# The order of TensorE's small products in two chunked recurrences: directions, heads and blocks in turn over the array's parts

## The chip, the core and the metric

The kernel runs on one core of one Trainium2 chip. The metric is the device time of one launch in microseconds (us). A launch is the whole inference step of a two-layer network, so every number below stands against a kernel of over 3 ms, of which the change touches one stage.

## The reference, cut to what matters

The reference takes 128 context tokens and 512 sample tokens of width 1024 through two layers. Layer 0 is SwiGLU, then a mixer with two parallel groups of heads (RWKV-7 with 8 heads of 64, and a gated DeltaNet with 4 heads of 128), then SwiGLU. Layer 1 has attention and a long convolution in the mixer's place. Both recurrences of layer 0 go over the tokens forwards and backwards, and the two outputs are added. All is fp32. RWKV's recurrence, and DeltaNet's with its triangular solve, are:

```python
def wkv7_scan(r, w, k, v, kk, a, S0):
    def step(S, xs):
        r_t, w_t, k_t, v_t, kk_t, a_t = xs
        sk = jnp.einsum('bhvk,bhk->bhv', S, kk_t)
        S = (S * w_t[:, :, None, :] - sk[..., None] * (kk_t * a_t)[:, :, None, :]
             + v_t[..., None] * k_t[:, :, None, :])
        return S, jnp.einsum('bhvk,bhk->bhv', S, r_t)
...
y_f, S_f = wkv7_scan(rh, hd(decay[:, :, 0]), hd(k_dir[:, :, 0]), vh, kk, hd(a[:, :, 0]), S0[:, 0])
y_b, S_b = wkv7_scan(fl(rh), fl(hd(decay[:, :, 1])), fl(hd(k_dir[:, :, 1])), fl(vh), fl(kk), ...)
y = y_f + fl(y_b)
...
T = lax.linalg.triangular_solve(eye + lower, jnp.broadcast_to(eye, lower.shape),
                                left_side=True, lower=True, unit_diagonal=True)
```

The kernel computes both in chunks of 64 tokens. Inside a chunk the step by step update becomes the inverse of a 64x64 unit triangular matrix (for every chunk, head and direction) and a few small matrix products; between chunks a state of 64x64 (RWKV) or 128x128 (DeltaNet) is carried.

## The kernel before, in words

**Layout.** 640 tokens are ten chunks of 64 (NCH = 10; CH = 64): two of context (PCH = 2), eight of sample. RWKV's heads go in four pairs: the two heads of a pair (hh = 0, 1) lie on partitions 0 to 63 and 64 to 127. A pair is worked on together with one DeltaNet head. Forward (d = 0) and backward (d = 1) go side by side: step s takes chunk c0 forwards and chunk c1 backwards. In the tiles that hold 64 tokens, direction 0 has one half of the partitions and direction 1 the other.

**TensorE's array and shapes.** All of the products here go through one helper, `mm` (L286–287), which is why the profile shows them all as L287; they are told apart by the names of their operands. The profile's row `ps<-VU,AT 64*64 64x64` is a product on a 64x64 part of the 128x128 array (64 rows hold the contraction, 64 columns the output's partitions), with 64 columns streamed. Which rows and which columns of the array follows from the partitions of the operands and of the output. An fp32 product is two weight loads and two MATMUL records. Results go to PSUM in banks of 128 x 512 words, and from there an engine copies them to SBUF. In this stage there are eight banks by tags (L962): two "ma", one "mt", one "mj", two "mc" (RWKV's steps), two "mg" (DeltaNet's steps).

**The functions that the change touches.**
- `rwkv_prep` (L1033), once for each head pair. At L1107–1115 it makes the lower triangular matrices L: 40 products of 64x64 (the profile's `w,w`), ten to a PSUM bank, four banks one after another, each masked by VectorE into L. A product's rows of the array are its head's half, its columns its direction's half.
- `inverses` (L1128), once for each head pair, as a generator in two parts. The 32x32 diagonal blocks are inverted by VectorE and GpSimd; the second part (L1185–1208) makes the off-diagonal blocks with 32x32 products: first `RL·rn` and `LT·gn` (the profile's `L,iv`/`iv,L` and `LT,gn`/`gn,LT`), a negated copy by ScalarE (zr, zg), then the products of zr and zg, and copies back by VectorE. RWKV's have ten products (chunks) for one 32x32 part of the array in a row, DeltaNet's have five.
- `rwkv_step` (L1244), for each of ten chunks of each pair: 40 steps. 36 of them have an incoming state S, four have none. Its parts: masked products AT (L1265–1268) and transposes E; then **AT·VU + Z·S** (L1281–1287), which is copied to B by VectorE for d = 0 and by ScalarE for d = 1; then **XT·B** (L1289–1293, the profile's `B,L`), copied to VU by ScalarE with a change of sign; then E·VU, which gives the new state S2 (L1295–1306); then the output **y** = Z·S + VU·AT (L1308–1321), added to ys. AT·VU uses 64 rows of the array (one direction's tokens) and 64 columns; Z·S uses all 128 rows (both heads, zeros in one of them) and 64 columns.

**What sets the order.** `mixers0` (L917–1015) writes the order of the stage out by hand: `advance((0,), n - LAP)`, `prepare(2)`, `advance((0, 1), LAP)`, `tail(0)`, and so on; `prepare` calls rwkv_prep, DeltaNet's preparation and the first part of `inverses`, and the second part of the pair before. The generator `chunks` (L1212) runs `gdn_step` (L1515, DeltaNet's step) and `rwkv_step` in turn, one part (up to a `yield`) of each. What that writes is not the last word: the kernel is built under `TileContext(nc, schedule_with_timeline_sim=True)` (L2143), a planner that orders each engine's instructions by a simulated timeline of its own. So the order in the trace can differ from the order in the code, and does: a product of DeltaNet stands between the two directions' blocks in some steps.

Of the kernel before, what the change touches and what calls it, by code (L numbers as in the profile page):

```python
# [9 lines left out]
ALU = mybir.AluOpType  # L10
# [3 lines left out]
P = 128  # L14
# [22 lines left out]
CH = 64  # L37
NCH = T // CH
# [220 lines left out]
class K:  # L259
# [773 lines left out]
    def rwkv_prep(self, hp, xp):  # L1033

        nc, I, ra = self.nc, self.I, self.ar
# [4 lines left out]
        r, k, kr, v = [self.wl() for _ in range(4)]  # L1040
# [6 lines left out]
        q = self.both(blk, sq, "ma")  # L1047
# [14 lines left out]
        L = self.t(xp, [P, 2 * NCH, CH], "L")  # L1062
        eG = self.t(xp, [P, 2, NCH], "eG")
        sa = []
        for d in range(2):
            sig, a = self.w(), self.w()
            for i, (b, out) in enumerate((("w0", sig), ("a0", a))):
                q = self.both(lora[:, 2 * i + d], self.wad[i], "ma")
                for c in range(2):
                    o = ch(out[:, c * H:c * H + H])  # L1070
# [3 lines left out]
        PQ, ks = [], []  # L1074
# [29 lines left out]
        at, _ = CONST["rmask"]  # L1104
        mask = self.const[:, at:at + CH].unsqueeze(1)
        n = NCH // 2
        for g in range(0, 2 * NCH, n):  # L1107
            hh, c0 = divmod(g, NCH)
            hr = slice(64 * hh, 64 * hh + 64)
            q = self.ps("ma")  # L1110
            for i in range(n):
                for d in range(2):
                    self.mm(q[64 * d:64 * d + 64, CH * i:CH * i + CH], PQ[d][1][hr, c0 + i], PQ[d][0][hr, c0 + i])
            nc.vector.tensor_tensor(out=L[:, g:g + n], in0=q[:, :n * CH].rearrange("p (u m) -> p u m", u=n),
                                    in1=mask.broadcast_to([P, n, CH]), op=ALU.mult)

        nc.vector.scalar_tensor_tensor(out=kds, in0=kds, scalar=self.col("r_k", hp), in1=r, op0=ALU.mult, op1=ALU.mult)
        q = self.both(blk, kds, "ma")
# [9 lines left out]
    def inverses(self, R, G):  # L1128
        nc, ra = self.nc, self.ar
        NP = NCH // 2  # L1130
        RL, LT = R["L"], G["LT"]
        g0, r0 = 4 * NP, 8 * NP
        nb = r0 + 8 * NCH
        dr = [self.t(self.dp, [nb, 32, 32], f"bl{i}") for i in range(3)]
        gv = lambda t, e: t[g0 * e:g0 * e + g0].rearrange("(b z c) s t -> b z s c t", b=2, z=2)
        rv = lambda t: t[r0:].rearrange("(b h c) s t -> b h s c t", b=2, h=2)
        quad = lambda hi, b: slice(64 * hi + 32 * b, 64 * hi + 32 * b + 32)
        cb = lambda b: slice(32 * b, 32 * b + 32)
        for b in range(2):
            for u in range(2):  # L1140
                nc.sync.dma_start(out=rv(dr[0])[b, u], in_=RL[quad(1 - u, b), :, cb(b)])
                for e in range(2):
                    nc.sync.dma_start(out=gv(dr[0], e)[b, u], in_=LT[quad(u, b), e, :, cb(b)])
        iv = lambda shape: self.t(ra, shape, "iv", bufs=4)
        L = [iv([nb, 16, 32]) for _ in range(2)]
        for i in range(2):
            nc.sync.dma_start(out=L[i][g0:], in_=dr[0][g0:, 16 * i:16 * i + 16])
        raw = [iv([g0, 16, 32]) for _ in range(2)]
        for i in range(2):
            nc.sync.dma_start(out=raw[i], in_=dr[0][:g0, 16 * i:16 * i + 16])  # L1150
        for i in range(2):
            for j in range(2):
                nc.scalar.copy(out=L[i][:g0, :, 16 * j:16 * j + 16], in_=raw[j].rearrange("p t s -> p s t")[:, 16 * i:16 * i + 16])
        xs = []
        for j0, nj, eng in ((0, NPOOL, nc.gpsimd), (NPOOL, 32 - NPOOL, nc.vector)):
            X = self.t(ra, [nb, nj, 32], f"X{j0}")
            flat = X.rearrange("p a b -> p (a b)")
            nc.gpsimd.memset(flat, 0.0)
            nc.gpsimd.memset(flat[:, j0::33], 1.0)
            self.invert_blocks(eng, L, X, j0, self.t(ra, [nb, 192], "inv", bufs=2))  # L1160
            nc.sync.dma_start(out=dr[1][:, j0:j0 + nj], in_=X)
            xs.append((X, j0))
        for i in range(2):
            xt = iv([nb, 16, 32])
            for X, j0 in xs:
                nc.scalar.copy(out=xt[:, :, j0:j0 + X.shape[1]], in_=X.rearrange("p s t -> p t s")[:, 16 * i:16 * i + 16])
            nc.sync.dma_start(out=dr[2][:, 16 * i:16 * i + 16], in_=xt)
        yield

        rn = iv([P, 2 * NCH, 32])  # L1170
        gn = self.t(ra, [P, NP, 32], "gn")
        for b in range(2):
            for u in range(2):
                nc.sync.dma_start(out=RL[quad(1 - u, b), :, cb(b)], in_=rv(dr[1])[b, u])
                for e in range(2):
                    nc.sync.dma_start(out=LT[quad(u, b), e, :, cb(b)], in_=gv(dr[2 - e], e)[b, u])
        for u in range(2):
            nc.sync.dma_start(out=rn[quad(1 - u, 0)], in_=rv(dr[2])[0, u])
            for e in range(2):
                nc.sync.dma_start(out=gn[quad(u, 1 - e)], in_=gv(dr[1 + e], e)[1 - e, u])  # L1180

        zr, zg = iv([P, 2 * NCH, 32]), self.t(ra, [P, NP, 32], "zg")
        qv = lambda q, rr, n, at=0: q[rr, at:at + 32 * n].rearrange("p (c s) -> p c s", c=n)
        qr, qg = [self.ps("ma") for _ in range(2)], self.ps("mt")
        for d in range(2):  # L1185
            for u in range(2):
                lo, hi = quad(u, 0), quad(u, 1)
                for c in range(NCH):
                    self.mm(qv(qr[d], hi, NCH)[:, c], RL[lo, NCH * d + c, 32:], rn[lo, NCH * d + c])
                nc.scalar.activation(out=zr[hi, NCH * d:NCH * d + NCH], in_=qv(qr[d], hi, NCH), func=AF.Copy, scale=-1.0)  # L1190
        for e in range(2):
            for z in range(2):
                lo, hi = quad(z, 1 - e), quad(z, e)
                for c in range(NP):
                    self.mm(qv(qg, hi, NP)[:, c], LT[lo, e, c, cb(e)], gn[lo, c])
        nc.scalar.activation(out=zg, in_=qv(qg, slice(None), NP), func=AF.Copy, scale=-1.0)
        for d in range(2):
            for u in range(2):
                lo, hi = quad(u, 0), quad(u, 1)
                for c in range(NCH):  # L1200
                    self.mm(qv(qr[d], lo, NCH)[:, c], zr[hi, NCH * d + c], RL[hi, NCH * d + c, 32:])
                nc.vector.tensor_copy(out=RL[lo, NCH * d:NCH * d + NCH, 32:], in_=qv(qr[d], lo, NCH))
        for e in range(2):
            for z in range(2):
                lo, hi = quad(z, 1 - e), quad(z, e)
                for c in range(NP):
                    self.mm(qv(qg, lo, NP, 32 * NP)[:, c], zg[hi, c], LT[hi, e, c, cb(e)])
                nc.vector.tensor_copy(out=LT[lo, e, :, cb(e)], in_=qv(qg, lo, NP, 32 * NP))
        yield

# [33 lines left out]
    def rwkv_step(self, X, ys, c0, c1, S, first):  # L1244

        nc, rt = self.nc, self.rt
        ZD, XD, XT, eG = [X[n] for n in ("ZD", "XD", "L", "eG")]
        ident = self.con("ident")
        pair = slice(c0, NCH + c1 + 1, NCH + c1 - c0)
        hrs = [slice(64 * hh, 64 * hh + 64) for hh in range(2)]  # L1250
        dc = [(0, c0), (1, c1)]
# [4 lines left out]
        Z, B = self.zeroed[self.zi % len(self.zeroed)]  # L1256
# [5 lines left out]
        mask = self.const[:, at:at + P].unsqueeze(1).broadcast_to([P, 4, P])  # L1262
        AT = self.t(rt, [P, 2, 2, P], "AT", bufs=3)
        q = self.ps("mj")
# [4 lines left out]
        q = self.ps("mj")  # L1269
# [4 lines left out]
        VU = self.t(rt, [P, 2, P], "VU", bufs=3)  # L1274
# [3 lines left out]
        for d, c, r, u in rows:  # L1278
            nc.scalar.copy(out=VU[r, d], in_=q[r, 2 * P:3 * P])
        yield  # L1280
        q = self.ps("mc")  # L1281
        for d, c, r, u in rows:
            for hh, hr in enumerate(hrs):
                self.mm(q[r, hr], AT[r, d, hh, :CH], VU[r, d, hr], stop=S is None)
                if S is not None:
                    self.mm(q[r, hr], Z[:, d, hh, :CH], S[:, d], start=False)
            (nc.vector.tensor_copy, nc.scalar.copy)[d](out=B[r, d], in_=q[r, :P])
        yield
        q = self.ps("mc")  # L1289
        for d, c, r, u in rows:  # L1290
            for hh, hr in enumerate(hrs):
                self.mm(q[u, hr], XT[:, NCH * hh + c], B[:, d, hr])
            nc.scalar.activation(out=VU[u, d], in_=q[u, :P], func=AF.Copy, scale=-1.0)
        S2 = self.t(rt, [P, 2, CH], "S", bufs=NSB)
        for d, c in dc:  # L1295
            yield
            q = self.ps("mc")
# [8 lines left out]
                nc.vector.scalar_tensor_tensor(out=S2[:, d], in0=q[:, :CH], scalar=e, in1=Se, op0=ALU.mult, op1=ALU.add)  # L1306
        yield
        q = self.ps("mc")  # L1308
        for hh, hr in enumerate(hrs):
            for d, c in dc:  # L1310
                o = q[hr, CH * d:CH * d + CH]
                if S is not None:
                    self.mm(o, S[:, d], Z[:, d, hh, CH:], stop=False)
                self.mm(o, VU[:, d, hr], AT[:, d, hh, CH:], start=S is None)
        for d, c in dc:
            to, x = ys[:, CH * c:CH * c + CH], q[:, CH * d:CH * d + CH]
# [830 lines left out]
```

## Time and profile before

| What | us |
|---|---|
| Median of three runs | 3269.26 |
| Fastest and slowest of them | 3264.29, 3270.95 |
| The profiled execution | 3277.03 |
| Its span in the profile | 3275.3 |
| Recurrence stage, looked at as a window of it | 900 to 1340 |

The profiled execution is one launch, 7.8 us above the median; durations from it are summed against its own time. TensorE's mean granted clock in it is 0.954 of full speed.

How to read the profile: PE is TensorE's MATMUL, PEld its weight loads, DVE is VectorE, ACT is ScalarE, POOL is GpSimd, SP the engine that issues DMAs. A row of a timeline gives the start, the length from the first start to the last end, engine, line, operation, out<-in by the program's names, the part of the array and the tile, and how many records were merged into it; in brackets the idle time before it and what ended it. The ends of MATMUL records are modelled and overlap the next record's start, so what one costs is read from its start to the next one's. A row of a window gives busy time and records of each engine and the granted TensorE clock. A row of a group gives the number of records, their busy time, the mean length in ns and the engine's idle time before them with what ended it.

### The profile page before, as it was taken

Reading aid. Unit: us, or ns where it says so; the run is one execution under the profiler, and the core shown is the slowest. Engines: PE = TensorE matmul, PEld = TensorE weight load, DVE = VectorE, ACT = ScalarE, POOL = GpSimd, SP = SyncE. Lnnn points to the kernel's source line nnn. Section 1 sums busy time; section 2 is a strip of 40 time slices with the busy share of each in tenths; the row PEclk is TensorE's granted clock in tenths of the full one; section 3 lists DMA queues with packets and bytes.
Section 4 is the critical chain, followed back from the end, with each engine's and each line's share of the span. In section 5 each row is a group of like instructions: output and inputs, shape, how many; then the busy total and the mean of one; then the engine's idle time right before and its main releaser. Section 6 shows DMA issues by size and latency. Waiting matters only on the chain.

```text
span 3275.3 us, 56038 instructions
## 1 busy us (share of the span) xinstructions
PE 3076.1 (94%) x21505; PEld 2751.9 (84%) x21505; DVE 2253.8 (69%) x3995; ACT 1378.2 (42%) x2876; POOL 1210.5 (37%) x1110
## 2 busy tenths in 40 slices
PE   7899999998899999889999979999989998899998
PEld 2799999987767777688999979999978846899998
DVE  5956667568567554586666787677766686877777
ACT  2423334676455444442333453333544423533333
POOL 4723334236424120153334555444410012544442
PEclk9999999999878888899999989999989998899999
DMA  7455433456444222426554232222321124222222
GB/s 261 160 187 179 161 127 97 157 167 169 132 119 112 66 77 69 141 96 204 163 167 149 71 98 96 78 85 84 93 94 54 58 75 163 71 95 80 78 91 81
DMA packets 277588, 385.37 MB, mean 118 GB/s; under 512 B 128704, under 2 KB 161120, under 8 KB 275400
## 3 DMA queue, kind: packets, MB, share of 16 engines
q1 hardware_dynamic: 277160, 381.13, 36.9%
q8 instruction: 169, 2.77, 0.3%
q14 instruction: 99, 0.81, 0.1%
q0 software_dynamic: 160, 0.66, 0.0%
HBM read 330.29 MB, written 51.42 MB: 117 GB/s over the span
## 4 chain that ended last, share of the span: by engine, by line
PE 58%; DVE 11%; DMA 3%; ACT 2%; issue 2%; POOL 1%; SPq 1%; DVEq 0%; ACTq 0%; POOLq 0%
PE ps L287 57%; DMA wr<-in_wd_dram 1%; DVE wl L655 1%; DVE b L605 1%; DVE wl L471 1%; DVE X L826 1%; DVE nx L539 0%; DMA wr<-in_wo_dram 0%; DVE inv L824 0%; PE ps L1750 0%; PE ps L1271 0%; POOL X L826 0%; DVE hidl L476 0%; DVE nacc L506 0%; POOL inv L824 0%
## 5 line engine op out<-in xcount | busy, mean ns | idle before, releaser
L287 PE MATMUL ps<-hh,wh 128*128 128x320 f32 x2208 | 695.6, 317 | 13.0 <-ACT hh L545 5.6
L287 PE MATMUL ps<-hl,wh 128*128 128x320 f32 x2208 | 692.1, 314 | 3.0 <-POOL hl L546 2.9
L287 PE MATMUL ps<-hh,wl 128*128 128x320 f32 x2208 | 681.9, 313 | 4.9 <-DVE wl L471 4.7
L287 PE MATMUL ps<-b,wh 128*128 128x320 f32 x2112 | 479.9, 314 | 39.4 <-DVE b L605 21.8
L287 PEld LDWEIGHTS ps<-hh,wh 128*128 128x128 f32 x2208 | 419.9, 191 | 28.1 <-issue 8.4
L287 PEld LDWEIGHTS ps<-hl,wh 128*128 128x128 f32 x2208 | 420.1, 190 | 8.0 <-POOL hl L546 4.4
L287 PEld LDWEIGHTS ps<-hh,wl 128*128 128x128 f32 x2208 | 417.7, 190 | 8.4 <-DVE wl L471 5.8
L287 PEld LDWEIGHTS ps<-b,wh 128*128 128x128 f32 x2112 | 360.2, 191 | 47.3 <-DVE b L605 23.8
L287 PE MATMUL ps<-hidl,wh 128*128 128x320 f32 x1248 | 383.2, 309 | 0.0
L287 PE MATMUL ps<-hidh,wh 128*128 128x320 f32 x1248 | 382.6, 312 | 0.0
L287 PE MATMUL ps<-hidh,wl 128*128 128x320 f32 x1248 | 381.2, 309 | 0.3 <-DVE wl L471 0.3
L550 DVE SCALAR_TENSOR_TENSOR x<-ps,mod,x 128x128 f32<-128x128 f32 (+2 forms) x528 | 212.6, 434 | 226.5 <-PE ps L287 221.1
L655 POOL TENSOR_TENSOR wl<-S,wh 128x512 fp32r<-128x512 f32 x176 | 256.1, 1455 | 274.1 <-ACT wh L654 271.3
L684 POOL TENSOR_TENSOR S<-wr,wu 128x512 f32<-128x512 f32 x88 | 129.3, 1470 | 589.5 <-DMA wr<-in_wgu_dram 364.5
L287 PE MATMUL ps<-b,wl 128*128 128x320 f32 x1056 | 329.6, 314 | 10.7 <-DVE wl L655 9.2
L470 ACT CAST wh<-wr 128x512 fp32r<-128x512 f32 (+2 forms) x210 | 157.7, 754 | 397.8 <-PE ps L287 308.8
L654 ACT CAST wh<-S 128x512 fp32r<-128x512 f32 (+1 forms) x264 | 201.3, 764 | 233.0 <-PE ps L287 175.6
L287 PEld LDWEIGHTS ps<-hidh,wh 128*128 128x128 f32 x1248 | 232.7, 188 | 13.2 <-issue 7.4
L471 DVE TENSOR_TENSOR wl<-wr,wh 128x512 fp32r<-128x512 f32 (+2 forms) x210 | 188.0, 898 | 80.0 <-ACT wh L470 78.0
L287 PEld LDWEIGHTS ps<-hidl,wh 128*128 128x128 f32 x1248 | 233.9, 188 | 0.0
L287 PEld LDWEIGHTS ps<-hidh,wl 128*128 128x128 f32 x1248 | 233.2, 188 | 0.7 <-DVE wl L471 0.6
L287 PEld LDWEIGHTS ps<-b,wl 128*128 128x128 f32 x1056 | 201.8, 192 | 13.7 <-DVE wl L655 11.2
(455 smaller groups left out, 6272.0 us busy)
## 6 DMA issues: line engine op xcount, KB each, us to landing
wmod<-in_wmod_dram SPq DMA_DIRECT2D x288, 256.0 KB, 5.0
wr<-in_wgu_dram SPq DMA_DIRECT2D x108, 512.0 KB, 3.4
wu<-in_wgu_dram SPq DMA_DIRECT2D x88, 512.0 KB, 4.3
wr<-in_wd_dram SPq DMA_DIRECT2D x80, 320.0 KB, 3.0
wr<-in_wd_dram SPq DMA_DIRECT2D x96, 256.0 KB, 2.7
pd<-o SPq DMA_DIRECT2D x32, 320.0 KB, 3.1
wr<-in_abg_dram SPq DMA_DIRECT2D x17, 512.0 KB, 6.5
wr<-in_wo_dram SPq DMA_DIRECT2D x16, 512.0 KB, 4.7
```

The costliest lines, as they stand in the source:

```text
L287: self.nc.tensor.matmul(out=out, lhsT=lhsT, rhs=rhs, start=start, stop=stop)
L470: nc.scalar.copy(out=wh, in_=w)
L471: nc.vector.tensor_sub(out=wl, in0=w, in1=wh.bitcast(F32))
L550: self.nc.vector.scalar_tensor_tensor(out=self.x[c][:, d, a:b], in0=q[:, a:b], scalar=gate[:, cond, d:d + 1], in1=self.x[c][:, d, a:b], op ...
L605: lo = v.tensor_sub(out=to[1], in0=r, in1=to[0].bitcast(F32))
L654: nc.scalar.copy(out=hi, in_=r)
L655: eng.tensor_tensor(out=lo, in0=r, in1=f32(hi), op=ALU.subtract)
L684: G.tensor_tensor(out=out, in0=x, in1=y, op=op)
L826: eng.tensor_tensor(out=X[:, :a, t], in0=X[:, :a, t], in1=tm, op=ALU.subtract)
```

## The change

The same products are issued in another order, and the copies out of PSUM behind some of them come later. Nothing is added or left out, and no sum is taken in another order within one output, except that in y the two heads' products are interleaved (each output still has Z·S first, VU·AT second).

- Preparation: two "ma" banks are held at once, one for each head. For each chunk the four products of both directions and both heads follow one another, over all four quarters of the array; then both banks are masked.
- Inverses: the chunk is the outer loop; the 32x32 parts (u for RWKV, e and z for DeltaNet) take turns within it. The copies come after all products of the group.
- AT·VU + Z·S: for each head, AT·VU for d = 0 and d = 1, then Z·S for d = 0 and d = 1; the copies to B of both directions come after both heads.
- XT·B: heads outside, directions inside; both copies after all four.
- y: directions outside; for each, Z·S for both heads, then VU·AT for both heads.

```diff
--- before.py
+++ after.py
@@ -1104,15 +1104,17 @@
         at, _ = CONST["rmask"]
         mask = self.const[:, at:at + CH].unsqueeze(1)
         n = NCH // 2
-        for g in range(0, 2 * NCH, n):
-            hh, c0 = divmod(g, NCH)
-            hr = slice(64 * hh, 64 * hh + 64)
-            q = self.ps("ma")
+        for c0 in range(0, NCH, n):
+            qs = [self.ps("ma"), self.ps("ma")]
             for i in range(n):
                 for d in range(2):
-                    self.mm(q[64 * d:64 * d + 64, CH * i:CH * i + CH], PQ[d][1][hr, c0 + i], PQ[d][0][hr, c0 + i])
-            nc.vector.tensor_tensor(out=L[:, g:g + n], in0=q[:, :n * CH].rearrange("p (u m) -> p u m", u=n),
-                                    in1=mask.broadcast_to([P, n, CH]), op=ALU.mult)
+                    for hh, q in enumerate(qs):
+                        hr = slice(64 * hh, 64 * hh + 64)
+                        self.mm(q[64 * d:64 * d + 64, CH * i:CH * i + CH], PQ[d][1][hr, c0 + i], PQ[d][0][hr, c0 + i])
+            for hh, q in enumerate(qs):
+                g = NCH * hh + c0
+                nc.vector.tensor_tensor(out=L[:, g:g + n], in0=q[:, :n * CH].rearrange("p (u m) -> p u m", u=n),
+                                        in1=mask.broadcast_to([P, n, CH]), op=ALU.mult)
 
         nc.vector.scalar_tensor_tensor(out=kds, in0=kds, scalar=self.col("r_k", hp), in1=r, op0=ALU.mult, op1=ALU.mult)
         q = self.both(blk, kds, "ma")
@@ -1182,29 +1184,37 @@
         zr, zg = iv([P, 2 * NCH, 32]), self.t(ra, [P, NP, 32], "zg")
         qv = lambda q, rr, n, at=0: q[rr, at:at + 32 * n].rearrange("p (c s) -> p c s", c=n)
         qr, qg = [self.ps("ma") for _ in range(2)], self.ps("mt")
+
         for d in range(2):
+            for c in range(NCH):
+                for u in range(2):
+                    lo, hi = quad(u, 0), quad(u, 1)
+                    self.mm(qv(qr[d], hi, NCH)[:, c], RL[lo, NCH * d + c, 32:], rn[lo, NCH * d + c])
             for u in range(2):
-                lo, hi = quad(u, 0), quad(u, 1)
-                for c in range(NCH):
-                    self.mm(qv(qr[d], hi, NCH)[:, c], RL[lo, NCH * d + c, 32:], rn[lo, NCH * d + c])
+                hi = quad(u, 1)
                 nc.scalar.activation(out=zr[hi, NCH * d:NCH * d + NCH], in_=qv(qr[d], hi, NCH), func=AF.Copy, scale=-1.0)
-        for e in range(2):
-            for z in range(2):
-                lo, hi = quad(z, 1 - e), quad(z, e)
-                for c in range(NP):
+        for c in range(NP):
+            for e in range(2):
+                for z in range(2):
+                    lo, hi = quad(z, 1 - e), quad(z, e)
                     self.mm(qv(qg, hi, NP)[:, c], LT[lo, e, c, cb(e)], gn[lo, c])
         nc.scalar.activation(out=zg, in_=qv(qg, slice(None), NP), func=AF.Copy, scale=-1.0)
         for d in range(2):
+            for c in range(NCH):
+                for u in range(2):
+                    lo, hi = quad(u, 0), quad(u, 1)
+                    self.mm(qv(qr[d], lo, NCH)[:, c], zr[hi, NCH * d + c], RL[hi, NCH * d + c, 32:])
             for u in range(2):
-                lo, hi = quad(u, 0), quad(u, 1)
-                for c in range(NCH):
-                    self.mm(qv(qr[d], lo, NCH)[:, c], zr[hi, NCH * d + c], RL[hi, NCH * d + c, 32:])
+                lo = quad(u, 0)
                 nc.vector.tensor_copy(out=RL[lo, NCH * d:NCH * d + NCH, 32:], in_=qv(qr[d], lo, NCH))
+        for c in range(NP):
+            for e in range(2):
+                for z in range(2):
+                    lo, hi = quad(z, 1 - e), quad(z, e)
+                    self.mm(qv(qg, lo, NP, 32 * NP)[:, c], zg[hi, c], LT[hi, e, c, cb(e)])
         for e in range(2):
             for z in range(2):
-                lo, hi = quad(z, 1 - e), quad(z, e)
-                for c in range(NP):
-                    self.mm(qv(qg, lo, NP, 32 * NP)[:, c], zg[hi, c], LT[hi, e, c, cb(e)])
+                lo = quad(z, 1 - e)
                 nc.vector.tensor_copy(out=LT[lo, e, :, cb(e)], in_=qv(qg, lo, NP, 32 * NP))
         yield
 
@@ -1278,18 +1288,22 @@
         for d, c, r, u in rows:
             nc.scalar.copy(out=VU[r, d], in_=q[r, 2 * P:3 * P])
         yield
+
         q = self.ps("mc")
+        turns = [(hh, hr) + row for hh, hr in enumerate(hrs) for row in rows]
+        for a in range(0, 4, 2):
+            for hh, hr, d, c, r, u in turns[a:a + 2]:
+                self.mm(q[r, hr], AT[r, d, hh, :CH], VU[r, d, hr], stop=S is None)
+            if S is not None:
+                for hh, hr, d, c, r, u in turns[a:a + 2]:
+                    self.mm(q[r, hr], Z[:, d, hh, :CH], S[:, d], start=False)
         for d, c, r, u in rows:
-            for hh, hr in enumerate(hrs):
-                self.mm(q[r, hr], AT[r, d, hh, :CH], VU[r, d, hr], stop=S is None)
-                if S is not None:
-                    self.mm(q[r, hr], Z[:, d, hh, :CH], S[:, d], start=False)
             (nc.vector.tensor_copy, nc.scalar.copy)[d](out=B[r, d], in_=q[r, :P])
         yield
         q = self.ps("mc")
+        for hh, hr, d, c, r, u in turns:
+            self.mm(q[u, hr], XT[:, NCH * hh + c], B[:, d, hr])
         for d, c, r, u in rows:
-            for hh, hr in enumerate(hrs):
-                self.mm(q[u, hr], XT[:, NCH * hh + c], B[:, d, hr])
             nc.scalar.activation(out=VU[u, d], in_=q[u, :P], func=AF.Copy, scale=-1.0)
         S2 = self.t(rt, [P, 2, CH], "S", bufs=NSB)
         for d, c in dc:
@@ -1306,11 +1320,12 @@
                 nc.vector.scalar_tensor_tensor(out=S2[:, d], in0=q[:, :CH], scalar=e, in1=Se, op0=ALU.mult, op1=ALU.add)
         yield
         q = self.ps("mc")
-        for hh, hr in enumerate(hrs):
-            for d, c in dc:
-                o = q[hr, CH * d:CH * d + CH]
-                if S is not None:
+        for d, c in dc:
+            outs = [(q[hr, CH * d:CH * d + CH], hh, hr) for hh, hr in enumerate(hrs)]
+            if S is not None:
+                for o, hh, hr in outs:
                     self.mm(o, S[:, d], Z[:, d, hh, CH:], stop=False)
+            for o, hh, hr in outs:
                 self.mm(o, VU[:, d, hr], AT[:, d, hh, CH:], start=S is None)
         for d, c in dc:
             to, x = ys[:, CH * c:CH * c + CH], q[:, CH * d:CH * d + CH]
```

## The prediction

> **What bounds the kernel now.** I read the page first, for the engines' busy time and the chain of work that ended last.
>
> ```profile
> span 3275.3 us, 56038 instructions
> PE 3076.1 (94%) x21505; PEld 2751.9 (84%) x21505; DVE 2253.8 (69%) x3995; ACT 1378.2 (42%) x2876; POOL 1210.5 (37%) x1110
> PE 58%; DVE 11%; DMA 3%; ACT 2%; issue 2%; POOL 1%; SPq 1%; DVEq 0%; ACTq 0%; POOLq 0%
> ```
>
> TensorE is busy 94% of the span and carries 58% of the chain. That is an average over stages, and the change touches one: the recurrences (rwkv_step) with the preparation and inverses of the later head pairs between them. So the next view is busy time by window, over 900 to 1340 us, where all but the first recurrence steps and three of the four head pairs' inverses lie, and over pieces of it.
>
> ```profile
> 980.00:1000.00 20.00, 17.00 (x140) 12.38 (x140) 18.77 (x36) 14.76 (x34) 16.29 (x18) 0.80 0.44 108
> 1140.00:1180.00 40.00, 38.49 (x332) 28.12 (x329) 33.63 (x107) 23.56 (x77) 25.53 (x62) 0.96 0.28 77
> 1207.00:1248.00 41.00, 41.00 (x344) 31.32 (x344) 13.46 (x41) 9.09 (x30) 0.00 (x0) 0.50 0.06 16
> 1320.00:1340.00 20.00, 17.77 (x144) 12.66 (x143) 12.54 (x41) 6.49 (x19) 0.00 (x0) 0.92 0.01 2
> 900.00:1340.00 440.00, 427.76 (x3951) 316.32 (x3951) 261.25 (x733) 218.58 (x683) 91.39 (x199) 0.86 0.31 83
> ```
>
> The columns are length, then busy time (and records) of PE, PEld, DVE, ACT, POOL, then the granted clock. In the last row TensorE is busy 427.76 of 440 us: a TensorE stage, although its products are tiny. Three pieces are not clearly TensorE's: 980 to 1000 and 1140 to 1180 (VectorE 18.77 of 20 and 33.63 of 40) and 1320 to 1340 (TensorE 17.77 of 20, the last pair alone): 80 us, 18% of the stage. In 1207 to 1248 TensorE is never idle, and its clock is 0.50.
>
> What the time goes into shows on TensorE's timeline of one step.
>
> ```profile
> 1316.93 0.33 PE L287 MATMUL ps<-VU,AT 64*64 64x64 f32 x2
> 1317.19 0.33 PE L287 MATMUL ps<-S,Z 128*64 128x64 f32 x2
> 1317.44 0.33 PE L287 MATMUL ps<-VU,AT 64*64 64x64 f32 x2
> 1317.70 0.33 PE L287 MATMUL ps<-S,Z 128*64 128x64 f32 x2
> 1317.96 0.49 PE L287 MATMUL ps<-h,Kt 128*128 128x128 f32 x2
> 1318.40 0.33 PE L287 MATMUL ps<-VU,AT 64*64 64x64 f32 x2
> ...
> 1319.34 0.22 PE L287 MATMUL ps<-B,L 128*64 128x64 f32 x1
> 1294.39 0.28 PE L287 MATMUL ps<-Z,S 128*64 128x64 f32 x2
> 1294.50 0.28 PE L287 MATMUL ps<-AT,VU 128*64 128x64 f32 x2
> 1294.62 0.34 PE L287 MATMUL ps<-Z,S 128*64 128x64 f32 x4
> 1294.74 0.33 PE L287 MATMUL ps<-AT,VU 128*64 128x64 f32 x4
> 1294.91 0.28 PE L287 MATMUL ps<-Z,S 128*64 128x64 f32 x2
> 1295.03 0.28 PE L287 MATMUL ps<-AT,VU 128*64 128x64 f32 x2
> 1295.23 0.38 PE L287 MATMUL ps<-h,Kt 128*128 128x128 f32 x1
> ```
>
> One fp32 product is two records. Lengths overlap, so a product's cost is read from start to next start. Where the products keep one shape (128*64, from 1294.39 on) one costs 0.11 to 0.12 us. Where 64*64 and 128*64 alternate (from 1316.93 on) each costs 0.26: a change of shape costs about 0.14 us (0.255 less 0.116). And the block of direction 1 (1318.40) begins only after VectorE's copy of direction 0's result:
>
> ```profile
> 1318.07 0.28 DVE L1287 COPY B<-ps 64x128 f32<-64x128 f32 x1 [0.51 <-PE ps L287]
> ```
>
> It ends at 1318.35, 0.05 us earlier.
>
> **The change, part by part.** No instruction is added or removed; no DMA, and nothing on SP's or POOL's queue moves. The copies stay, but start later.
>
> *AT·VU and Z·S (L1281–1287).* Now four products for one direction (1316.93 to 1317.96: 1.03 us), a copy, four for the other (1318.40 to 1319.34: 0.94), eight products with eight changes of shape: 1.97. After: AT, AT, Z, Z, AT, AT, Z, Z, the two neighbours on opposite columns, the two AT also on opposite rows. What such a pair costs:
>
> ```profile
> 1280.54 0.43 PE L287 MATMUL ps<-Vt,LT 64*64 64x128 f32 x4
> 1280.90 0.48 PE L287 MATMUL ps<-Z,XV 128*128 128x256 f32 x1
> 1288.71 0.43 PE L287 MATMUL ps<-h,AQ 128*64 128x128 f32 x2
> 1289.08 0.33 PE L287 MATMUL ps<-VU,AT 64*64 64x64 f32 x2
> ```
>
> Two products Vt,LT (64*64 tiles on opposite rows and columns, one PSUM bank) take 0.36 us from start to next start; one product of the same 128 columns (h,AQ) takes 0.37. The second runs beside the first. The two Z,S products at 1294.62 likewise take 0.12, as one does. So four pairs at 0.26: 1.04, a saving of 0.93 us where a state comes in. How often:
>
> ```profile
> L287 PE MATMUL ps<-VU,AT 64*64 64x64 f32 x320 | 53.8, 256 | 1.4 <-DVE B L1287 0.6 <-DVE S L1306 0.6
> L287 PE MATMUL ps<-S,Z 128*64 128x64 f32 x288 | 50.8, 262 | 0.0
> ```
>
> 320 records are 160 products, 40 steps of four; 288 are 36 steps: 36 × 0.93 = 33.5 us. At half clock the block is dearer:
>
> ```profile
> 1214.04 0.47 PE L287 MATMUL ps<-VU,AT 64*64 64x64 f32 x2
> ...
> 1215.65 0.36 PE L287 MATMUL ps<-L,iv 32*32 32x32 f32 x3
> ```
>
> 1.61 us for the same four products, 1.56 times 1.03. A mean clock of 0.86 is 28% of the time at half, hence a fifth of the work; the saving times 1.1 is **37 us**. Bounds: 0 if the planner lays the blocks apart again, 42 if the pairs reach the 0.23 us that two same-shape products cost.
>
> *The y products (L1309–1313).* Now 0.84 us (1294.39 to 1295.23) with six alternations of operands; after: per direction two Z·S and two VU·AT on opposite columns, four pairs. By the pair at 1294.62 (0.12) and the one at 1294.74 (0.17) that is 0.57 in all: 0.27 × 36 = **10 us**; between 0 and 13 (0.12 for each pair).
>
> *XT·B (L1289–1293).* Four products in one visit in place of two visits. A visit between other shapes costs up to two changes, 0.28; where its neighbours have its shape, nothing. 40 steps × 0 to 0.28 is 0 to 11; **5**, the middle, since the row at 1319.34 has a same-shape neighbour on one side.
>
> *Inverses (L1185–1208).* 32*32 products; now ten or five of one tile in a row, after: two or four tiles in turn.
>
> ```profile
> 819.02 1.35 PE L287 MATMUL ps<-iv,L 32*32 32x32 f32 x37 [0.62 <-DMA iv<-bl]
> 1116.12 1.15 PE L287 MATMUL ps<-gn,LT 32*32 32x32 f32 x40
> 1117.19 0.48 PE L287 MATMUL ps<-Z,XV 128*128 128x256 f32 x1
> ```
>
> iv,L: 37 records in about 1.2 us (0.032 each); gn,LT: 40 in 1.07 with a small overlap where the tile changes. A head pair has 160 records of the first kind and 80 of the second, four pairs 960. With two side by side: 640 × 0.016 + 320 × 0.012 = 14 us; with four in the gdn part up to 18; nothing if records already come as fast as they are issued. I take **8**, nearer to the iv,L row, where no neighbours overlap today. The Trainium skill ("TensorE: Matmul & The Clock Gate") states that starts of matmuls never come closer than about 25 ns however few the columns. By it the 0.032 can fall only to 0.025, the term would be an estimated 4 us, and the total 4 us less; the trace agrees so far, since its closest records, gn,LT's, come at 1.07/40 = 0.027 us.
>
> *Preparation (L1107–1115).*
>
> ```profile
> 696.42 1.78 PE L287 MATMUL ps<-w,w 64*64 64x64 f32 x54 [0.20 <-DVE w L1094]
> ```
>
> 54 records in 1.6 us, about 0.03 each, columns already in turn. The change adds turns over rows: 320 records × 0 to 0.015 is 0 to 4.7; **2**, since no row shows two row tiles over the same columns. Holding two banks "ma" at once delays the first mask by about one bank's products (0.6 us), four head pairs: nothing, as VectorE is not TensorE's wait there (0.20 us in that row is the only one).
>
> *Sum.* 37 + 10 + 5 + 8 + 2 = 62 us on TensorE. In 80 of 440 us (18%) another engine sets the pace; there it gives nothing: 62 × 0.82 = 51. In those steps the copies' new place costs: direction 0's copy, now at 1317.96, waits for the other direction's four products, some 0.5 us; behind it on VectorE stand gdn's updates of state and output and the masks of the next AT, which wait too, and for them gdn's next products. 36 × 0.18 × 0.5 = 3 us. In the other steps gdn's products (h,Kt at 1317.96) cover it; without that cover it is 36 × 0.5 = 18 us. Late next is ScalarE's copy of VU, after XT. Net **48 us**. The profiled execution took 3277.03 us (span 3275.3 and 1.7 around it), so 3229 by its own time; it lies 7.8 above the median 3269.26 of the three runs, from which the forecast is 3221.
>
> **Rivals.**
>
> *The chain of a step becomes the bound (slower gain).* Today direction 1's products run while direction 0 is copied; after, both directions copy at the same time and TensorE has only gdn's products. If that cover is gone, AT/Z and XT give nothing, and what stays is y, inverses and preparation: 20 us, 3249. For: idle is already charged to DVE's B and S in the VU,AT row; against: 1.2 us in all, and TensorE is idle 12 of 440 us.
>
> *The clock.* 28% of the stage, 123 us, runs at half clock though TensorE is busy (1207 to 1248). Tiny products fill a quarter or a sixteenth of the array; packed closer, the array is used more per us. If two thirds of that time goes to full clock, 123 × 0.67 × (1 − 1/1.56) = 30 us more: 78, 3191; all of it gives some 15 more, and with the upper bounds of the terms about 3155. For: 1140 to 1180, with as many records per us, has 0.96. Against: packing gains some 11% of density.
>
> *Slower: row tiles that share a bank take turns.* In the inverses (L1189–1207) neighbours now lie on different rows of the array and write one bank. If each of 480 such turns drains the array as a change of shape does, 0.14 us, that is +67; the AT pairs lose half of their gain, so 16 of T1, with 10 and 5, is left: net +36, 3305. It decides from 31/480 = 0.065 us a turn. The Vt,LT row speaks against it: opposite rows, one bank, no turn. The Trainium skill ("TensorEngine Tiling (Array Packing)", Restrictions and Gotchas) says that different row tiles cannot access the same PSUM bank at once; by that rule, the time would be 3305, and the trace's Vt,LT pair does not agree with it.
>
> *No change.* The planner orders each engine by its own simulated time and may put gdn's products between the pairs as it put h,Kt at 1317.96: changes of shape stay, 3269.
>
> **How the numbers follow.** Forecast (gain 25 to 75, 3194 to 3244) 0.64; clock 0.15; chain 0.12; no change 0.05; slower 0.04. Of the unknown terms, the lower ends together (0 for XT, inverses and preparation) leave a gain of about 35, the upper ends about 70; the range reaches to the chain's 3249 with some more lost, 3258, and past the clock's 3191 to 3168. Some 6 us (0.2%) is what a measurement can tell. Faster 0.91 (forecast, clock, chain), same 0.05, slower 0.04.
>
> **What would show it.** Right: in the group rows VU,AT and S,Z with mean cost from start to start near 0.13 us, pairs x4 on the timeline; y near 0.57; B's two copies within 0.3 us of each other; stage some 48 shorter, other stages the same. Wrong: AT,Z in turn as now; iv,L above 0.032 a record; PE idle in 900 to 1300 above 25 us (chain); mean clock of the stage off 0.86 by more than 0.03 (clock).

## The result, and the profile after

The changed kernel takes 3221.14 us (median of four runs, 3200.98 to 3228.88) beside 3267.23 us before: a ratio of 0.983, 95% interval 0.9806 to 0.9854. Measured a second time, for an experiment below, it is 0.9821 (0.98 to 0.9841). The forecast was 3221, so 48 us less; 46 were measured, and 58 the second time (3214.34 beside 3271.97). The profiled execution took 3213.42 us, span 3211.6.

The page and busy time by window follow. The first window reaches from the first AT·VU product to DeltaNet's last product, the second from RWKV's last y product to there. The first fence is the kernel before, the second the changed one.

```profile
915.00:1347.00 432.00, 422.58 (x3925) 313.86 (x3925) 252.61 (x731) 206.95 (x656) 79.14 (x178) 0.86 0.31 82
1328.00:1347.00 19.00, 15.74 (x82) 10.55 (x79) 11.25 (x34) 6.68 (x19) 1.94 (x2) 0.82 0.13 41
```

```profile
PE 2995.3 (93%) x21505; PEld 2680.3 (83%) x21505; DVE 2254.6 (70%) x3995; ACT 1375.1 (43%) x2876; POOL 1206.8 (38%) x1110
...
915.00:1289.00 374.00, 351.38 (x3928) 251.10 (x3928) 253.00 (x731) 205.88 (x658) 79.71 (x179) 0.89 0.37 98
1251.00:1289.00 38.00, 30.43 (x130) 19.00 (x127) 18.78 (x57) 11.35 (x31) 2.26 (x2) 0.62 0.18 64
```

The stage has the same records (3925 and 3928) and the same work on VectorE and ScalarE, in 58 us less: the gain is in this stage. Three things are to be seen. TensorE's busy time fell by 71 us, but the stage by 58: idle time rose from 9.4 to 22.6 us. The clock rose from 0.86 to 0.89. And DeltaNet's steps after RWKV's last now take 38 us in place of 19, at a clock of 0.62.

The y group and the AT/Z group on the changed kernel's TensorE timeline, from two different steps:

```profile
1234.95 0.34 PE L287 MATMUL ps<-Z,S 128*64 128x64 f32 x4
1235.12 0.29 PE L287 MATMUL ps<-AT,VU 128*64 128x64 f32 x4
1235.23 0.29 PE L287 MATMUL ps<-Z,S 128*64 128x64 f32 x4
1235.35 0.29 PE L287 MATMUL ps<-AT,VU 128*64 128x64 f32 x4
1235.57 0.33 PE L287 MATMUL ps<-VU,AT 64*64 64x64 f32 x4
...
1227.95 0.33 PE L287 MATMUL ps<-VU,AT 64*64 64x64 f32 x4
1228.22 0.34 PE L287 MATMUL ps<-S,Z 128*64 128x64 f32 x4
1228.48 0.33 PE L287 MATMUL ps<-VU,AT 64*64 64x64 f32 x4
1228.74 0.34 PE L287 MATMUL ps<-S,Z 128*64 128x64 f32 x4
1228.91 0.39 PE L287 MATMUL ps<-const,XV 128*64 128x128 f32 x4
```

Pairs (x4) where single products stood (x2). The y group takes 0.62 us (1234.95 to 1235.57; 0.84 before), the eight products of AT/Z 0.96 us in one visit (1227.95 to 1228.91; 1.97 before). A pair costs 0.26, as one product did, where the shape changes behind it; the last costs 0.17, since the product that follows has its shape.

### The profile page after: what moved, and what is told of

The parts are those of the page before. It is cut to its first block, busy times and chain, and to the rows that moved or that the text cites. A ratio compares the mean times of both kernels' runs of the same rounds, so it can differ in the third digit from the quotient of the medians.

```text
span 3211.6 us, 56035 instructions
## 1 busy us (share of the span) xinstructions
PE 2995.3 (93%) x21505; PEld 2680.3 (83%) x21505; DVE 2254.6 (70%) x3995; ACT 1375.1 (43%) x2876; POOL 1206.8 (38%) x1110
## 4 chain that ended last, share of the span: by engine, by line
PE 53%; DVE 13%; DMA 4%; ACT 4%; issue 3%; POOL 1%; SPq 1%; DVEq 0%; ACTq 0%; POOLq 0%
PE ps L287 52%; DMA wr<-in_wd_dram 1%; DVE wl L655 1%; DMA wr<-in_wo_dram 1%; DVE nx L539 1%; DVE inv L824 1%; DVE wl L471 1%; DVE X L826 1%; DVE nacc L514 0%; PE ps L1765 0%; DMA pd<-o 0%; DVE b L605 0%; POOL X L826 0%; ACT wh L470 0%; DVE nx L710 0%
```

## The experiments

Each is a kernel of its own. To compare stages that ran at different clocks I use one number: the stage's length less 0.36 of its half-clock time, where half-clock time is length × 2 × (1 − clock), since the clock records of these traces hold only 1 and 0.5, and 0.36 is 1 − 1/1.56, the price of half clock that the prediction took from the 1214.04 block. I call it full-clock length. Before: 432 − 0.36 × 121 = 388; changed: 374 − 0.36 × 82 = 344.

**AT/Z alone.** The hunk of L1281–1287, the rest as before:

```diff
+        for a in range(0, 4, 2):
+            for hh, hr, d, c, r, u in turns[a:a + 2]:
+                self.mm(q[r, hr], AT[r, d, hh, :CH], VU[r, d, hr], stop=S is None)
...
         for d, c, r, u in rows:
...
             (nc.vector.tensor_copy, nc.scalar.copy)[d](out=B[r, d], in_=q[r, :P])
```

> Of the change, only the order AT, AT, Z, Z with both copies to B behind it. Theory (TensorE's time in the stage is what counts, and this edit is most of it): a step's eight products take about 1.0 us in place of 1.97, 27 us less in all (37 x 0.82 - 3), 19 to 35 with the clock's share. Rival (the clock: the gain comes from stretches that leave half clock, which need the whole change's packing): under 10 us, with the stage's half-clock time as before, some 125 us. Rival (a step's chain becomes the bound when both copies come late): 0 to 10 us, with TensorE idle in the stage up by 20 us or more.

**Inverses alone.** The hunk of L1185–1208:

```diff
+            for c in range(NCH):
+                for u in range(2):
...
-                for c in range(NCH):
...
```

> Of the change, only the inverses' turns over the 32x32 parts. Theory: the records come 16 ns apart where two parts take turns and 8 to 10 where four do, 16 us less TensorE time in four head pairs, of which three lie in the TensorE stage: 8 to 14 us less in all; the prediction's term was 7. Rival (row tiles that share a bank take turns): 30 to 67 us slower. Rival (the inverses wait on transfers and copies, and their products lie beside other work): 0 to 4 us.

**y alone.** The hunk of L1309–1313:

```diff
+            if S is not None:
+                for o, hh, hr in outs:
                     self.mm(o, S[:, d], Z[:, d, hh, CH:], stop=False)
+            for o, hh, hr in outs:
...
```

> Of the change, only the y products' order. Theory: the group takes 0.57 to 0.62 us in place of 0.85, 36 x 0.25 x 0.82 = 7 us less. Rival (y is at the end of a step and nothing on the chain waits for it; its time is filled from the other work's slack): within 3 us of before.

**XT and preparation alone.** The hunks of L1289–1293 and L1107–1115:

```diff
+        for hh, hr, d, c, r, u in turns:
+            self.mm(q[u, hr], XT[:, NCH * hh + c], B[:, d, hr])
...
+            qs = [self.ps("ma"), self.ps("ma")]
```

> Of the change, the XT products in one visit with both copies of VU behind them, and the preparation's turns. Theory by the prediction: 5 + 2, times 0.82: 6 us less. By the rows of the changed kernel, where XT's records come as far apart as before (63 ns) and the first XT product is often parted from the others: 0 to 3 us less. Rival (XT for direction 0 now waits for direction 1's copy before VU can be copied): up to 5 us slower.

Measured on one chip, before at 3275.63: AT/Z 3241.47 (ratio 0.9882, 0.9859 to 0.9904), inverses 3233.34 (0.9867, 0.9845 to 0.9888), y 3264.42 (0.9963, 0.9947 to 0.9979), XT and preparation 3255.85 (0.9936, 0.9918 to 0.9953). Gains of 34, 42, 11 and 20 us: 107 together, about twice the whole change. Only AT/Z's lies where it was expected (19 to 35); the other three gained more than theory or rival said. The stage's rows, in this order:

```profile
918.00:1307.00 389.00, 364.21 (x3928) 271.06 (x3927) 256.53 (x732) 204.93 (x657) 78.73 (x178) 0.91 0.35 94
```

```profile
918.00:1309.00 391.00, 379.03 (x3927) 280.14 (x3925) 252.19 (x731) 206.34 (x658) 80.15 (x178) 0.93 0.34 89
```

```profile
921.00:1351.00 430.00, 418.68 (x3927) 307.46 (x3927) 251.90 (x732) 206.86 (x657) 79.87 (x178) 0.85 0.31 82
```

```profile
917.00:1336.00 419.00, 403.28 (x3920) 296.42 (x3921) 248.88 (x729) 202.22 (x649) 78.84 (x176) 0.90 0.31 82
```

Full-clock lengths are 364, 371, 384 and 389, so 24, 17, 4 and −1 less than before: 44 in all, which is what the whole change has (388 − 344). The lengths add; the half-clock times do not: 121 us before, then 70, 55, 129 and 84, and 82 for all five edits together. Three of the four single edits already shift the work so that less of it runs at half clock; the 42 us of the inverses are 17 of packing and 24 of clock (0.36 × 66), and the 20 us of XT and preparation are clock alone.

Each of these lengths stands on one profiled execution, and AT/Z's was the fastest of its runs (3226.70, median 3241.47). The same sum can be made for every execution on record, over the whole kernel, from its span and mean clock. The mean gains at full clock are then 28 us (AT/Z), 16 (inverses), 5 (y) and 1 (XT and preparation), each to about 4 us: some 50 together, beside 46 for the whole change measured again below. So the lengths add here too. The factor 0.36 is an estimate from one block; between executions of one kernel, a us more at half clock made the span about 0.32 us longer, all kernels taken together. Of the clock, the inverses' share (219 to 227 us at half clock in the whole kernel) and that of XT and preparation (234 to 274) lie outside before's scatter of 275 to 329; those of AT/Z and y overlap it.

**The whole once more, and the whole without AT/Z.** The second kernel is the diff without its hunk of L1281–1287 (the line `turns = ...` stays, which XT uses).

> The whole change once more, beside the runs of parts of it on one chip. Single edits, each alone, gained 34 (AT/Z), 42 (inverses), 11 (y) and 20 us (XT and preparation), 107 together. Theory (the packed products add up, and the clock's gain is one and the same for each edit): 45 to 58 us less than before, so 3217 to 3230 where before takes 3275; not 107. Rival (the edits add up and the first measurement of the whole change was a poor one): 90 us or more.

> The whole change without the AT/Z edit. Theory: at full clock the stage shrinks by what the parts showed alone, 16 (inverses) + 5 (y) + 0 = 21 us, and the half-clock time of the stage, 125 us before, falls once, to 50 to 90: another 12 to 27, so 33 to 48 us less, no more than the inverses alone. Rival (gains of single edits add): 42 + 11 + 20 = 73 us less.

The whole: 3214.34 (before 3271.97), 58 less and not 107, at the upper end of what was expected; its stage, 371 us at a clock of 0.90, has the full-clock length 344 again. Without AT/Z: 3227.97 (0.9855, 0.9832 to 0.9879), 44 less, not 73. Its stage is 372 us at a clock of 0.98, so full-clock length 367: 21 less than before, where the parts alone give 17 + 4 − 1 = 20. Its half-clock time of 15 us lies below the 50 to 90 expected; the times and the full-clock lengths bear the theory out.

**Only the copies moved.** The order of products as before:

```diff
-            (nc.vector.tensor_copy, nc.scalar.copy)[d](out=B[r, d], in_=q[r, :P])
+        for d, c, r, u in rows:
+            (nc.vector.tensor_copy, nc.scalar.copy)[d](out=B[r, d], in_=q[r, :P])
```

> The kernel before, with the products of AT/Z in their old order (AT, Z, AT, Z for one direction, then the other), and only the copies to B of both directions moved behind all eight products. Theory (the gain lies in fewer changes of the array's shape and in pairs that run beside each other): the eight products still take 1.9 to 2.0 us; in time 0 to 5 us slower, by the copies' later start, unless the clock moves. Rival (the gain lies in direction 1's block not waiting for direction 0's copy): most of the AT/Z gain, 15 us or more at the same half-clock time.

3288.62 us, ratio 1.005 (1.0032 to 1.0068): 17 us slower, more than the 5 expected. The products now follow without a break, each still at 0.26:

```profile
1318.68 0.32 PE L287 MATMUL ps<-VU,AT 64*64 64x64 f32 x2
1318.93 0.33 PE L287 MATMUL ps<-S,Z 128*64 128x64 f32 x2
1319.19 0.33 PE L287 MATMUL ps<-VU,AT 64*64 64x64 f32 x2
1319.44 0.33 PE L287 MATMUL ps<-S,Z 128*64 128x64 f32 x2
...
1320.73 0.71 PE L287 MATMUL ps<-W,KQ 128*128 128x128 f32 x4
...
917.00:1360.00 443.00, 422.33 (x3926) 314.97 (x3926) 256.40 (x732) 205.90 (x656) 78.67 (x178) 0.85 0.31 82
```

2.05 us for eight products, full-clock length 395: 7 us longer than before (8 by all executions), the rest being clock. So AT/Z's gain is in the order of its products, and the copies' later start is its price.

**DeltaNet written one chunk ahead** (in the whole change, in `chunks`):

```diff
+        gs, rs = steps(self.gdn_step, W, (G,)), steps(self.rwkv_step, S, (R, y))
+        ahead = [next(gs)]
+        for to, j, g in ahead[0]:
+            for r in g:
...
+            ng, nr = next(gs, []), next(rs)
```

> The whole change, and DeltaNet's steps written one chunk ahead of RWKV's in the order that the planner is given. In the changed kernel the last RWKV step ends 38 us before DeltaNet's last step (19 us before the change), and 29 of these 38 us run at half clock. Theory (the wait moved to DeltaNet's chain at the end): that stretch falls to 20 us or less, and the whole gains 8 to 18 us on the changed kernel. Rival (the planner orders by its own simulated times, whatever the written order): the same within 5 us. Rival (the lead delays RWKV's chain at the start of each pair by one DeltaNet step): up to 10 us slower than the changed kernel.

3211.59 us (0.9812, 0.9791 to 0.9834), the same as the whole; the stretch after RWKV's last step is 39 us, not 20. The written lead did not reach the trace. The order of TensorE's records did change, but DeltaNet was no further ahead: when half of RWKV's records in the stage were done, 40% of DeltaNet's were, and 41% in the changed kernel. That the planner goes by its own times fits this; what a real lead would give is not shown.

**More products, against the clock.** In the kernel before, ahead of each group of a step:

```diff
         q = self.ps("mc")
+        self.mm(q[:, P:], self.reset[:, :P], self.reset[:, :3 * P])
```

> The kernel before, with one more product (bf16, 128x128 array, 384 columns, into columns of the bank that nothing reads) ahead of each of the five groups of an RWKV step: 200 products of an estimated 0.16 us at full clock, with changes of shape 0.3. Theory (the clock falls where too little of the array is used, though TensorE is busy): half-clock time from 915 us to the last DeltaNet step falls from 125 us to under 70, while the stage in full-clock time (its length less 0.36 of the half-clock time) grows by 30 to 60; so 10 to 45 us slower. Rival (the clock goes by TensorE's busy time, which is 98% already, or by something outside): half-clock time stays at 110 us or more, and it is 35 to 70 us slower.

3340.93 us, 67 slower than before (1.0201, 1.0155 to 1.0248). The stage is 494 us at a clock of 0.85: half-clock time 148, not under 70, 30% of the stage where it was 28%. Full-clock length is 441, 53 more, within the 30 to 60 expected. The added work did not lift the clock, so the theory that too little use of the array lowers it is not borne out at this dose; the other side's numbers came. What lowers it stays open.

**Neighbours in two banks** (in the whole change):

```diff
-        for d in range(2):
+        for x in range(2):
             for c in range(NCH):
                 for u in range(2):
-                    lo, hi = quad(u, 0), quad(u, 1)
+                    d, lo, hi = u ^ x, quad(u, 0), quad(u, 1)
...
```

> The whole change, with RWKV's inverse products in turns of direction 0's one part and direction 1's other part, so that neighbours lie in two PSUM banks and not in one; parts of the array, counts and copies as in the change. Theory (neighbours on opposite rows and columns run beside each other in one bank already): the records come 16 to 18 ns apart as in the change. Rival (row tiles that share a bank take turns): they come closer than in the change, 12 ns or less.

One execution, 3221.11 us. The records' mean distance is 19 to 20 ns, beside 17 to 18 in one bank (mean over starts of successive records of one kind at full clock): no closer. A shared bank costs nothing here.

**AT pair, Z pair, Z pair, AT pair** (in the whole change):

```diff
+            for k in (0, 1) if a == 0 else (1, 0):
                 for hh, hr, d, c, r, u in turns[a:a + 2]:
...
```

> The whole change, with the AT/Z group in the order AT pair, Z pair, Z pair, AT pair, one change of the array's shape less in each of 36 steps (each output is still the sum of its two products). Theory (a change of shape costs 0.14 us): the group takes about 0.85 us in place of 0.96 to 1.04, 36 x 0.14 x 0.82 = 4 us less than the change, so 3210 beside 3214 where before takes 3272, and the second Z pair's start comes 0.12 us after the first's. Rival (the price is a change of operands, or the accumulation, not of shape): the same group time, no gain.

The first fence has the changed kernel's group of Z·S (busy us, then mean ns of a record), the second this one's, and its timeline.

```profile
L287 PE MATMUL ps<-S,Z 128*64 128x64 f32 x288 | 26.3, 257 | 0.0
```

```profile
L287 PE MATMUL ps<-S,Z 128*64 128x64 f32 x288 | 18.8, 248 | 0.0
...
1239.63 0.45 PE L287 MATMUL ps<-S,Z 128*64 128x64 f32 x8
```

Two Z pairs in 0.45 us where one alone has 0.34: the second costs about 0.11, so the price is that of a change of shape. Yet the time is 3219.78 (0.9844, 0.982 to 0.9867), not clear of the whole's, and the full-clock length 384 − 0.36 × 108 = 345 is the same. TensorE is idle 26.6 us in the stage, 4 more than in the changed kernel: what it saved went idle. So TensorE's busy time at full clock no longer sets this stage alone.

**The whole without the XT edit** (L1289–1293 as before):

```diff
-        for hh, hr, d, c, r, u in turns:
-            self.mm(q[u, hr], XT[:, NCH * hh + c], B[:, d, hr])
         for d, c, r, u in rows:
+            for hh, hr in enumerate(hrs):
+                self.mm(q[u, hr], XT[:, NCH * hh + c], B[:, d, hr])
```

> The whole change without the XT edit: XT products of one direction, its copy of VU, then the other's. By the prediction: 5 x 0.82 = 4 us slower than the change. By the runs so far (XT and preparation alone: 0 us at full clock): the same within 3 us of the change, at the same half-clock time. Rival (direction 0's VU copy comes earlier again, and the chain with it): up to 5 us faster.

3195.62 us (0.9774, 0.9753 to 0.9794): faster than the whole change (0.9821, 0.98 to 0.9841, on another chip, each beside the kernel before on its own). The intervals do not meet, and the gain is more than either side expected.

```profile
916.00:1270.00 354.00, 329.27 (x3927) 238.97 (x3927) 249.00 (x733) 205.58 (x658) 82.37 (x178) 0.95 0.39 103
1245.00:1270.00 25.00, 19.72 (x92) 12.30 (x91) 15.29 (x48) 8.24 (x24) 2.26 (x2) 0.87 0.24 74
```

Full-clock length 354 − 0.36 × 35 = 341, 3 us less than the whole; the half-clock time is 35 in place of 82, worth 17. By all executions the gain at full clock is 43 us on before, no more than the 46 of the whole, so that the earlier copy gains anything is not shown. The gain is the clock's: 204 or 205 us at half clock in the whole kernel in each of the four executions, 244 to 276 in the five of the whole. Of the clock it can only be said where it changed: the stretch behind RWKV's last step is 25 us at a clock of 0.87, not 38 at 0.62.

## Why the prediction was right, step by step

- *The bound.* Right: the stage held the gain, and full-clock lengths added up edit by edit, as time on one engine does. The prediction's window of 900 to 1340 us does not lack the first recurrence steps, as it says: they begin at 915, and what it lacks is DeltaNet's last 7 us.
- *AT/Z.* Right. 0.96 us for 1.04 forecast; alone 24 us of full-clock length, and the forecast without its tenth for half clock is 33.5 × 0.82 − 3 = 24.5. The parts were apart from the forecast's: the late copies cost 7 (forecast 3), so the order gave some 31 (forecast 27.5).
- *y.* Right in the group, 0.62 us for 0.57; alone it gave 4 us, half of the 10 × 0.82 = 8 forecast.
- *XT.* Wrong: "40 steps × 0 to 0.28 is 0 to 11; 5, the middle". The visits were joined in part: counted over the traces, XT's records stand in 139 visits before and in 80 after, of which 14 hold a step's eight records. And joining saves little: at full clock a record cost 63 ns from start to next start before and 59 after, 320 × 0.004 = 1 us. In the step shown here direction 1's copy to B, which is ScalarE's, comes later, behind two others of its own:

```profile
1229.13 0.28 DVE L1301 COPY B<-ps 64x128 f32<-64x128 f32 x1 [1.22 <-PE ps L287]
...
1229.78 0.26 ACT L1301 COPY B<-ps 64x128 f32<-64x128 f32 x1
1229.81 0.33 PE L287 MATMUL ps<-B,L 128*64 128x64 f32 x2
1231.13 0.45 PE L287 MATMUL ps<-B,L 128*64 128x64 f32 x6
```

  One XT product goes, then TensorE takes other work, and direction 0's copy of VU, before ready after its own two products, waits for all four. XT and preparation together gave −1 by the profiles and 1 by all executions, for 7 × 0.82 = 6 forecast. Preparation came as forecast: 54 records took 1.30 us to the next start (779.00 to 780.30) where 54 took 1.71, so 320 save some 2 us, half of them ahead of the stage.
- *Inverses.* The mechanism was right, the term too small: 8 taken, 0 to 18 stated, 17 measured.

```profile
823.07 1.36 PE L287 MATMUL ps<-L,iv 32*32 32x32 f32 x74
824.24 0.22 PE L287 MATMUL ps<-LT,zg 32*32 32x32 f32 x2
...
1076.08 0.43 PE L287 MATMUL ps<-gn,LT 32*32 32x32 f32 x26
```

  74 records in 1.17 us (0.016 each, 0.032 before) with two parts in turn; 26 in some 0.24 (0.43 less the 0.19 that one lasts), 0.009 each, with four. So four head pairs save about 640 × 0.016 + 320 × 0.018 = 16 us, and the three in the stage 12; the 17 lies above that by about the scatter of the measurement. With two parts the starts alternate, 6 to 7 ns and 25 ns: two records in the 32 ns of one. The prediction stayed low because no neighbours overlapped in its iv,L row. Its "closest records" at 0.027 us were a mean of two kinds: in the same trace gn,LT's starts at full clock come down to 5 to 6 ns around a change of the part and are mostly 25 to 32 ns apart elsewhere, so the overlap could have been read there. The rule from the Trainium skill ("TensorE: Matmul & The Clock Gate", section "Wait — 56ns, not 53.3ns?") of about 25 ns between starts does not hold for records on different parts of the array.
- *Slower by shared banks.* Did not come. The rule of the Trainium skill ("TensorEngine Tiling (Array Packing)", Restrictions and Gotchas) on row tiles in one bank does not agree with the L,iv rows, whose neighbours lie on different rows of the array in one bank, nor with the run of two banks, which brought them no closer.
- *The factor 0.82.* Without the tenth for half clock the prediction's sum is (33.5 + 10 + 5 + 8 + 2) × 0.82 − 3 = 45 us, beside 44 measured. That it fits so well is luck: the inverses gave 10 us more than their 7, and y, XT and preparation 11 less than their 14. Nor did the factor stand for VectorE's stretches alone: the end, where DeltaNet's steps run alone, grew from 19 to 38 us, 11 of them at full clock (16.5 to 27.6).
- *The chain as a rival.* It was there in part. TensorE's idle time rose from 3.3 to 7.6 us in the end, and before RWKV's last product from 6.2 to 15.1 (the first fence is before, the second after):

```profile
915.00:1328.00 413.00, 406.84 (x3848) 303.31 (x3849) 241.36 (x698) 200.28 (x637) 77.19 (x176) 0.86 0.32 84
```

```profile
915.00:1251.00 336.00, 320.95 (x3802) 232.09 (x3802) 234.22 (x675) 194.53 (x627) 77.45 (x177) 0.92 0.39 101
900.00:1300.00 400.00, 366.50 (x3987) 260.33 (x3986) 272.57 (x760) 225.16 (x706) 94.79 (x205) 0.88 0.37 99
```

  By the prediction's own sign for it, more than 25 us idle in 900 to 1300, it came: 33.5, though that window now reaches past the stage's end, and the stage itself has 22.6. Its price did not come: AT/Z, which it said would give nothing, gave 24. B's two copies, named to begin within 0.3 us of each other, begin 0.65 apart in the step above and 0.31 to 0.34 in half of the steps.
- *The clock.* The rival came in part: half-clock time 121 to 82 us, worth 14. In the profiled pair 44 + 14 = 58 is the stage's gain; the rest of the kernel was 6 us shorter. The forecast counted on no change of the clock, so that the median of the first measurement fell on 3221 is in part luck: the four runs of the changed kernel lie 28 us apart, with clocks from 0.967 (3200.98) to 0.955 (3228.87), and the second measurement gained 58.

## What to carry to other kernels

Where many small products fill TensorE, read what one costs from start to next start, in its place: a change of the array's shape doubled the price here, and a neighbour on other columns came free. Joining two visits of TensorE gave little here: the operands of both have to be ready together, so look at which engine makes the later one. And before single edits are added up, take the clock out: the lengths at full clock added, the measured gains counted the clock's gain more than once.

## What the runs showed of the hardware that was not expected

Records on two parts of the array began 16 ns apart on average in one visit, 17 to 18 over the whole trace, and on four parts 9 ns, all in one PSUM bank; in two banks they came no closer (19 to 20). In the stage before, the clock was at half for stretches of 3.4 to 41 us, and in the longest (1207 to 1248) TensorE was busy all the time. Reordering moved these stretches: half-clock time of the stage lay between 15 us (without AT/Z) and 133 us (copies moved) for the same work, and 200 added products did not lower it.
